# Hybrid mLSTM and dilated-attention layer: order-only edges between PSUM evictions, weight splits and one GpSimd product

## The chip, the cores and the metric

The kernel runs on one core of a Trainium2 chip. A core has five engines that run side by side, each with its own in-order stream of instructions: TensorE (PE in the profile, with PEld for its weight loads), VectorE (DVE), ScalarE (ACT), GpSimd (POOL) and SyncE (SP, which here only issues DMAs). They wait for one another through semaphores. Matrix products land in PSUM, in banks of 128 partitions by 512 floats, and a bank can be used again only after its content has been read out ("evicted") by VectorE or ScalarE. The metric is device time in microseconds of one launch, the median of several runs.

## The reference

One encoder layer is applied to two inputs with shared weights: batch A (x_prompt, 1024 positions) and batch B (x_sample, 512 positions), both 1024 wide. Everything is float32.

```python
h = rms_norm(x, pre_w)
cols = einsum('bsd,dc->bsc', h, w_in)          # one wide projection
m_qk, m_v, m_o, m_z, m_i, m_f, a_qkv, a_z, gate = split(cols)
y_m = mlstm_mixer(m_qk, ...) * silu(m_z)       # 4 heads x 256, forwards and backwards, chunks of 128
y_a = dilated_attention(a_qkv, ...) * silu(a_z) # 3 groups (window, dilation) x 8 heads x 64
p_m, p_a = y_m @ w_pm, y_a @ w_pa
merged = sigmoid(gate[0]) * p_m + sigmoid(gate[1]) * p_a
out = x + rms_norm(merged @ w_out, post_w)
```

`mlstm_mixer` runs a short convolution with SiLU over q and k and then, for each head and direction, a chunked scan. In each chunk the scores q·k are weighted by exponentials of the gates, multiplied with v ("num"), the state matrix's part (q times state) is added, and the state is brought up to date: state = decay * state + k·v ("kv").

## The kernel before, in words

Every float32 product on TensorE is made from three products in a faster 32-bit format: `mm3` (L209 to L211) multiplies high by high, high by low and low by high. So each operand is split first: the high part is a rounded copy, the low part the difference. For weights that is `split_w`, a copy on ScalarE (L272, called wh in the profile) and a subtraction on VectorE (L278, wl). Splits of activations work the same way (Hh and Hl, sch and scl, qh and ql, kh and kl, ch and cl).

*Part 1* (0 to about 950 us). The projection of A and B together, by a scheme with seven products of quarter blocks instead of eight, named B11, T2, B21, T3, T1, T4, B22 in the code. First come the value columns, in groups (`value_group`): the weights' sums are split by its inner `split` (high on ScalarE L477, low on VectorE L478, tiles vhi and vlo). In the first group the sums of the input are still being made beside it by `put` (`combos`): TensorE transposes or adds blocks, ScalarE copies the high part Hh (L432), VectorE subtracts the low part Hl (L434), four column blocks k = 0 to 3 for each sum. While product T3 runs, `with_m7` puts T1's and then T2's input; product T2 comes next and reads it; the split of `s[:, 0]` (`s1`) is for the product after that, T1. In this part the order on all engines but TensorE is made by a scheduler.

*Part 2* (from about 950 us). The order on TensorE and SyncE is written out by hand. Four stages run one after another: `mlstm` for A (to about 1310 us), `attend` for A (to about 1640), `mlstm` for B (to about 1810), `attend` for B (to about 2075), then what is left of the final projections. Each stage has gaps in which TensorE would wait, and these are filled from one queue, `Fill`, with *dense units*: eight steps of `mm3` that add into one PSUM bank (tile `dense`), taken in steps by `fill(share)`. Units are B's remaining projections (`short_units`, with the weights of one 128-column block of w_in each), the value columns (`value_units`), the two branch projections (`branches`) and the output projection (`final`). A unit ends with `use`, which evicts the bank:

- attention's q and k (`att_unit`): high on ScalarE L772, low on VectorE L774
- convolution units: a copy on ScalarE L870 and then `conv_unit` (L735 on ScalarE, L737 and L739 on VectorE)
- SiLU units (`silu`): tanh on ScalarE L746, product on VectorE L749 or L751, the latter also reading a value kept from an earlier unit
- merge gates: tanh on ScalarE L896
- branch projections: VectorE L1643 and L1661
- output projection: square on ScalarE L1704, product on VectorE L1706 or L1711

There are two dense banks (four in the tail), so a third unit cannot begin before the first is evicted. `Fill.load` splits the weights of a unit two to four places ahead of its use; the call that does it comes in program order around the eviction of an earlier unit. The raw weights arrive in `wraw`, loaded on SyncE's queue or (w_pm, w_out and some of w_v) on GpSimd's.

In part 2 the order on ScalarE, VectorE and GpSimd is still the scheduler's, led by its own model of how long things take. `issue_after(x)` adds an edge to it: what is issued in this context comes after x. Such an edge costs no instruction. Some edges stand already: `held` keeps the splits behind the last evictions of the value units and of attention, `scans` keeps the low half of a split behind the last two updates of the mLSTM's state and output.

In `mlstm`, `front(k)` makes a round's operands: `rm` is masked on GpSimd (L1103), exponentiated on ScalarE (L1105) and multiplied with the scores on VectorE (L1106); `sch` (ScalarE L1109) and `scl` (GpSimd L1110) are its halves; `qw` (GpSimd L1114) is q times a row vector that a broadcast load brings (`rw`), and `qh` (ScalarE L1117) and `ql` (GpSimd L1118) are its halves; `kh` (ScalarE L1124) and `kl` (VectorE L1125) are k's. `core(k)` makes the num product, the kv product, updates the state `cf` (VectorE L1149 in a head's first chunk, L1152 later), adds the state's part, and evicts num as X (ScalarE L1167 in the first half of the chunks, VectorE L1169 in the second). `ch` (ScalarE L1176) and `cl` (VectorE L1177) are the state's halves.

## Time and profile before

| | |
|---|---|
| Median of three runs | 2258.14 us (2256.8 to 2259.2) |
| Profiled execution, own time | 2261.5 us |
| Its span in the trace | 2259.7 us |
| TensorE busy | 2244.2 us (99%) |
| VectorE busy | 1509.5 us (67%) |
| ScalarE busy | 1129.2 us (50%) |
| GpSimd busy | 718.6 us (32%) |
| Granted TensorE clock | 1.00 |

The own time of the profiled execution is 1.8 us longer than the span, which goes from the first to the last instruction in the trace. It lies 3.4 us above the median of the runs. A row of the timeline has the start in us, the duration in us, the engine, the line of the kernel, the operation, the result and the operands by the program's names, the shapes and how many of them were joined in the row; in brackets stands the idle time of the engine before it and what ended that. Matmuls are pipelined: of two that follow without a pause the second starts well before the first one's end in the trace, so pauses are read from start to start.

### The profile page before, as it was taken

To read this page: it belongs to the slowest core of one execution; us is meant where nothing else is said; L and a number is where in the kernel's file an instruction comes from. 1 tells how busy PE (TensorE), PEld (TensorE's weight loads), DVE (VectorE), ACT (ScalarE), POOL (GpSimd) and SP (SyncE) were. 2 spreads that over 40 slices of the span, in tenths; PEclk is the share of its full clock that TensorE was granted. 3 is DMA by queue.
4 is the path that set the end of the run, shared out by engine and by line. 5 is a ranking of instruction groups with operands and counts; after the bars stand their busy time and mean duration, and the time that the engine had idled before them with its cause. 6 is when DMAs were issued, how large, how long until landed. Compare 5 with 4: busy or idle time off the path is not lost.

```text
span 2259.7 us, 35388 instructions
## 1 busy us (share of the span) xinstructions
PE 2244.2 (99%) x12226; PEld 1964.6 (87%) x12226; DVE 1509.5 (67%) x2875; ACT 1129.2 (50%) x2369; POOL 718.6 (32%) x1000
## 2 busy tenths in 40 slices
PE   9999999999999999999999999999999999999998
PEld 8999888888888888888888899999888888888887
DVE  7765577687776556558887755544689844655674
ACT  6432244344444434357777655566665644554332
POOL 1000333333333223237676610011165522221221
PEclk9999999999999999999999999999999999999999
DMA  3652455543332223284664789997678797776663
GB/s 123 168 134 76 172 205 192 192 176 121 112 111 103 84 84 140 103 298 153 226 223 127 191 217 235 253 245 221 203 248 284 238 278 211 233 251 200 233 230 109
DMA packets 222685, 418.27 MB, mean 185 GB/s; under 512 B 24841, under 2 KB 128969, under 8 KB 222506
## 3 DMA queue, kind: packets, MB, share of 16 engines
q1 hardware_dynamic: 194536, 315.86, 44.4%
q0 software_dynamic: 24368, 87.56, 12.4%
q10 hardware_dynamic: 3602, 12.59, 1.4%
q8 instruction: 97, 1.59, 0.3%
q14 instruction: 82, 0.67, 0.1%
HBM read 296.19 MB, written 128.12 MB: 188 GB/s over the span
## 4 chain that ended last, share of the span: by engine, by line
PE 95%; DMA 2%; issue 1%; ACT 1%; POOL 1%; DVE 0%; DVEq 0%; SPq 0%; POOLq 0%; ACTq 0%
PE d L211 14%; PE d L209 14%; PE d L210 14%; PE dense L209 12%; PE dense L211 12%; PE dense L210 12%; PE o L1398 4%; PE pt L1385 2%; PE lg L1362 2%; PE num L211 1%; PE num L209 1%; PE num L210 1%; PE kv L209 1%; PE a L1070 1%; PE kv L210 1%
## 5 line engine op out<-in xcount | busy, mean ns | idle before, releaser
L209 PE MATMUL dense<-H,wh 128*128 128x512 f32 x664 | 270.6, 408 | 0.8 <-DVE V0b L1643 0.8
L211 PE MATMUL dense<-H,wl 128*128 128x512 f32 x664 | 260.9, 393 | 0.0
L210 PE MATMUL dense<-H,wh 128*128 128x512 f32 x664 | 260.2, 392 | 0.0
L210 PE MATMUL d<-Hl,phla 128*128 128x512 f32 x608 | 236.5, 389 | 0.0
L211 PE MATMUL d<-Hh,phla 128*128 128x512 f32 x608 | 236.5, 389 | 0.0
L209 PE MATMUL d<-Hh,phla 128*128 128x512 f32 x608 | 236.5, 389 | 0.0
L278 DVE TENSOR_TENSOR wl<-wraw,wh 128x1024 fp32r<-128x1024 f32 (+1 forms) x121 | 149.3, 1234 | 70.0 <-ACT wh L272 69.9
L1374 DVE CUSTOM_DVE_ANT_0 ls<-lg,bias 128x256 f32<-128x256 f32 (+1 forms) x288 | 93.7, 362 | 132.8 <-PE lg L1362 71.2
L211 PE MATMUL d<-Hh,phlb 128*128 128x512 f32 x456 | 177.4, 389 | 0.0
L209 PE MATMUL d<-Hh,phlb 128*128 128x512 f32 x456 | 177.4, 389 | 0.0
L210 PE MATMUL d<-Hl,phlb 128*128 128x512 f32 x456 | 177.4, 389 | 0.0
L687 POOL TENSOR_TENSOR psum_w<-pw_raw 128x512 f32<-128x512 f32 x38 | 58.0, 1527 | 365.1 <-DMA pw_raw<-w_in 208.8
L1378 ACT ACTIVATE ls<-ls,nm 128x256 f32<-128x256 f32 (+1 forms) x288 | 130.3, 454 | 84.0 <-DVE nm L1376 59.2
L272 ACT ACTIVATE wh<-wraw 128x1024 fp32r<-128x1024 f32 (+1 forms) x124 | 128.7, 1038 | 77.1 <-PE dense L210 27.0
L211 PEld LDWEIGHTS dense<-H,wl 128*128 128x128 f32 x664 | 124.6, 188 | 28.2
L209 PE MATMUL d<-vhi,Hh 128*128 128x322 f32 x448 | 140.9, 315 | 0.3
L211 PE MATMUL d<-vhi,Hl 128*128 128x322 f32 x448 | 140.3, 313 | 0.4 <-DVE Hl L396 0.2
L210 PE MATMUL d<-vlo,Hh 128*128 128x322 f32 x448 | 139.7, 312 | 0.0
L209 PEld LDWEIGHTS dense<-H,wh 128*128 128x128 f32 x664 | 125.0, 188 | 15.5 <-DVE V0b L1643 1.2
L210 PEld LDWEIGHTS dense<-H,wh 128*128 128x128 f32 x664 | 125.4, 189 | 14.3
L211 PEld LDWEIGHTS d<-Hh,phla 128*128 128x128 f32 x608 | 114.1, 188 | 23.7
L210 PEld LDWEIGHTS d<-Hl,phla 128*128 128x128 f32 x608 | 114.2, 188 | 23.6
(570 smaller groups left out, 6166.4 us busy)
## 6 DMA issues: line engine op xcount, KB each, us to landing
pw_raw<-w_in SPq DMA_DIRECT2D x76, 512.0 KB
wraw<-w_in SPq DMA_DIRECT2D x64, 512.0 KB
aqk_a<-pwk SPq DMA_DIRECT2D x48, 512.0 KB
aqk_b<-sw SPq DMA_DIRECT2D x48, 256.0 KB
wraw<-w_pm POOLq DMA_DIRECT2D x24, 512.0 KB, 6.1
wraw<-w_out POOLq DMA_DIRECT2D x24, 512.0 KB, 4.0
wraw<-w_v POOLq DMA_DIRECT2D x22, 430.0 KB, 7.3
erep<-erow SPq DMA_DIRECT2D x16, 512.0 KB
```

Of the source, the lines that this page charges most:

```text
L209: nc.tensor.matmul(out, lh, rh, start=start, stop=False)
L210: nc.tensor.matmul(out, lh, rl, start=False, stop=False)
L211: nc.tensor.matmul(out, ll, rh, start=False, stop=stop)
L272: high = nc.scalar.activation(hi[:, :n], raw[:, :n], AF.Copy)
L278: low = (self.lows or nc.vector).tensor_sub(lo[:, :n], raw[:, :n], hi[:, :n].bitcast(F32))
L687: self.nc.gpsimd.tensor_add(s[:, 0], ws[1][:, 0], ws[1][:, 1])
L1070: nc.tensor.matmul(p[:, c - c0], kT[:, ct, c * P:(c + 1) * P], qT[:, ct, c * P:(c + 1) * P], start=ct == 0, stop=ct == 1)
L1362: nc.tensor.matmul(lg[:, hh, c:c + w], q[hh][:, qs], z[:, k0:k0 + w], start=z is k[hh], stop=z is not k[hh])
L1374: nc.vector.tensor_tensor_reduce(out=ls[:, hh], in0=ts["lg"][hh], in1=bt[:, hh], scale=1.0, scalar=NEG, op0=OP.add, op1=OP.max, accum_out= ...
L1378: self.held = self.held[-3:] + [nc.scalar.activation(ls[:, hh], ls[:, hh], AF.Exp, bias=nm[:, hh:hh + 1], accum_out=ot[:, 128 + hh:129 + hh])]
L1385: nc.tensor.transpose(pp[:, hh * nk + x], ts["ls"][:, hh, x * P:(x + 1) * P], self.ident)
L1398: nc.tensor.matmul(po[:, hh * 64:hh * 64 + 64], pt[:, hh * nk + x], v[:, kt[x], c0 + hh * 64:c0 + hh * 64 + 64], start=x == 0, stop=x == n ...
```

## The change

The change adds order edges only; no instruction is added, taken away or altered.

1. Each dense unit notes its eviction's instructions in `self.evicted`, and both halves of the next weight split (`split_w`) are ordered behind them. For the branch projections and the two halves of SiLU only the reads of the bank are noted as shown.
2. In the first eight rounds of an mLSTM stage GpSimd's `qw` is ordered behind `scl`.
3. In the first value group the split of `s[:, 0]` is ordered behind the last copy L432 of T2's input (`top`), beside the edge that it had (`low[2]`, the subtraction of the same block).

```diff
-        self.low_part = None
+        self.low_part, self.evicted = None, []
...
 def split_w(self, raw, n):
...
-            for x in self.held:
+            for x in (*self.held, *self.evicted):
                 st.enter_context(self.tc.issue_after(x.ins))
             high = nc.scalar.activation(hi[:, :n], raw[:, :n], AF.Copy)
...
-                for x in (*self.held, *self.scans):
+                for x in (*self.held, *self.evicted, *self.scans):
                     st.enter_context(self.tc.issue_after(x.ins))
                 low = (self.lows or nc.vector).tensor_sub(lo[:, :n], raw[:, :n], hi[:, :n].bitcast(F32))
...
 def put(m, k):
...
-            nc.scalar.activation(hi, p, AF.Copy)
+            self.high = nc.scalar.activation(hi, p, AF.Copy)
...
             m7 = product(T3, split(wb[:, 0]), with_m7())
+            top = self.high
...
         if g == 0:
-            with self.tc.issue_after(low[2]):
+            with self.tc.issue_after(low[2]), self.tc.issue_after(top.ins):
                 s1 = split(s[:, 0])
...
 def silu(self, c, g, w):
...
-        nc.scalar.activation(th, c, AF.Tanh, scale=0.5)
+        self.evicted = [nc.scalar.activation(th, c, AF.Tanh, scale=0.5)]
         if g is None:
             g = th
-            nc.vector.scalar_tensor_tensor(g, th, 1.0, c, op0=OP.add, op1=OP.mult)
+            self.evicted.append(nc.vector.scalar_tensor_tensor(g, th, 1.0, c, op0=OP.add, op1=OP.mult))
...
 def att_unit(self, j, c, T, w):
...
-            nc.scalar.activation(h, x, AF.Copy, scale=1.0 if keys else 0.125)
+            self.evicted = [nc.scalar.activation(h, x, AF.Copy, scale=1.0 if keys else 0.125)]
...
+            low = nc.vector.scalar_tensor_tensor(l, x, 1.0 if keys else 0.125, h.bitcast(F32), op0=OP.mult, op1=OP.subtract)
+        self.evicted.append(low)
...
 def front(k):
...
-                nc.gpsimd.tensor_sub(scl, rm, sch.bitcast(F32))
+                low = nc.gpsimd.tensor_sub(scl, rm, sch.bitcast(F32))
...
                 if i > 0:
                     qw = sb.tile([P, 2, P], F32, name="qw")
-                    nc.gpsimd.tensor_tensor(qw, ...)
+                    with self.tc.issue_after(low.ins) if k < 8 else ExitStack():
+                        nc.gpsimd.tensor_tensor(qw, ...)
```

In the same way `self.evicted = [...]` is set at the evictions L870 (convolution), L896 (merge gate), L1643 and L1661 (branch projections), and at L1704 with L1706 or L1711 appended (output projection).

More of the change, by code (lines that the diff above doesn't have):

```diff
@@ L771, in att_unit @@
         for h, _, x in parts:
-            nc.scalar.activation(h, x, AF.Copy, scale=1.0 if keys else 0.125)
+            self.evicted = [nc.scalar.activation(h, x, AF.Copy, scale=1.0 if keys else 0.125)]
         for h, l, x in parts:
-            nc.vector.scalar_tensor_tensor(l, x, 1.0 if keys else 0.125, h.bitcast(F32), op0=OP.mult, op1=OP.subtract)
+            low = nc.vector.scalar_tensor_tensor(l, x, 1.0 if keys else 0.125, h.bitcast(F32), op0=OP.mult, op1=OP.subtract)
+        self.evicted.append(low)
         self.put(("aqk", T.S, j), T.aqk[0, j], hi.bitcast(F32), hi)
@@ L869, in use @@
             def use(p):
-                nc.scalar.activation(self.sraw[:, 1:1 + BLK], p, AF.Copy)
+                self.evicted = [nc.scalar.activation(self.sraw[:, 1:1 + BLK], p, AF.Copy)]
                 self.conv_unit(u, T, self.sraw, w, False)
@@ L895, in use @@
                 t = w()
-                nc.scalar.activation(t, p, AF.Tanh, scale=0.5)
+                self.evicted = [nc.scalar.activation(t, p, AF.Tanh, scale=0.5)]
                 self.put(("gt", T.S, br, ct), T.gt[br, ct], t, t)
@@ L1113, in front @@
                     qw = sb.tile([P, 2, P], F32, name="qw")
-                    nc.gpsimd.tensor_tensor(qw, x["q"][:, :, cs], rw[:, 1][:, None, :].to_broadcast([P, 2, P]), op=OP.mult)
+                    with self.tc.issue_after(low.ins) if k < 8 else ExitStack():
+                        nc.gpsimd.tensor_tensor(qw, x["q"][:, :, cs], rw[:, 1][:, None, :].to_broadcast([P, 2, P]), op=OP.mult)
                     qh = sb.tile([P, 2, P], F32R, name="qh")
@@ L1642, in proj_m @@
                     if k == KT - 1:
-                        nc.vector.scalar_tensor_tensor(m2[ct // 4][:, ct % 4], gates.pop((1, ct)), 1.0, pm, op0=OP.add, op1=OP.mult)
+                        self.evicted = [nc.vector.scalar_tensor_tensor(m2[ct // 4][:, ct % 4], gates.pop((1, ct)), 1.0, pm,
+                                                                       op0=OP.add, op1=OP.mult)]
                     yield
@@ L1659, in proj_a @@
                         mg = self.osb.tile([P, BLK], F32, name="mg", bufs=2)
-                        nc.vector.scalar_tensor_tensor(mg, gates.pop((0, ct)), 1.0, pa, op0=OP.add, op1=OP.mult)
+                        self.evicted = [nc.vector.scalar_tensor_tensor(mg, gates.pop((0, ct)), 1.0, pa, op0=OP.add, op1=OP.mult)]
                         nc.vector.tensor_add(mg, mg, m2[ct // 4][:, ct % 4])
@@ L1703, in close @@
                 o1 = sb.tile([P, BLK], F32, name="mg", bufs=2) if u else o[t]
-                nc.scalar.activation(o1, p, AF.Square, accum_out=ss[:, t, u:u + 1])
+                self.evicted = [nc.scalar.activation(o1, p, AF.Square, accum_out=ss[:, t, u:u + 1])]
                 if u == 0:
-                    nc.vector.tensor_mul(o[t], p, pw[:, c])
+                    self.evicted.append(nc.vector.tensor_mul(o[t], p, pw[:, c]))
                     return
@@ L1710, in close @@
                 nc.gpsimd.tensor_tensor(ss[:, t, 6:7], ss[:, t, 5:6], self.mhalf[:, :1], op=OP.pow)
-                nc.vector.tensor_mul(o1, p, pw[:, c])
+                self.evicted.append(nc.vector.tensor_mul(o1, p, pw[:, c]))
                 for hf, x in enumerate((o[t], o1)):
```

## The prediction

> **What bounds the kernel now.** I read the page's first part for the engine that bounds, the list of TensorE's waits for what a new order on the other engines could take away at all, and the timeline around each of those waits.

> ```profile
> PE 2244.2 (99%) x12226; PEld 1964.6 (87%) x12226; DVE 1509.5 (67%) x2875; ACT 1129.2 (50%) x2369; POOL 718.6 (32%) x1000
> L278 DVE TENSOR_TENSOR wl<-wraw,wh 128x1024 fp32r<-128x1024 f32 (+1 forms) x121 | 149.3, 1234 | 70.0 <-ACT wh L272 69.9
> ```

> ```profile
> core 0 of [0], span 2259.7 us
> PE d L1803 <- DMA Hh<-prew: 2.3, 1, 2.3
> PE num L211 <- POOL scl L1110: 1.2, 1, 1.2
> PE kv L209 <- DVE cf L1152: 1.2, 2, 0.6
> PE d L391 <- DVE u2b L389: 0.8, 1, 0.8
> PE dense L209 <- DVE V0b L1643: 0.8, 1, 0.8
> PE dense L209 <- ACT sw L896: 0.7, 1, 0.7
> PE d L438 <- ACT Hh L432: 0.5, 1, 0.5
> PE kv L209 <- DVE r L1163: 0.4, 1, 0.4
> PE o L1398 <- ACT pts L1388: 0.2, 1, 0.2
> PE num L209 <- DVE X L1169: 0.2, 1, 0.2
> PE d L211 <- DVE Hl L396: 0.2, 1, 0.2
> PE kv L209 <- DVE cf L1149: 0.2, 1, 0.2
> PE d L211 <- DVE Hl L434: 0.2, 1, 0.2
> ```

> TensorE works in 2244.2 of 2259.7 us. The second view gives the engine and line that waited, the writer it waited for, the total, the count and the longest. All thirteen together are 8.9 us. No matmul is added, removed or moved by the change, so what it can win is part of these 8.9 us, and what it can lose is a new entry in this list. VectorE and ScalarE have a third and a half of the span free; their order matters only where a result of theirs is late for TensorE.

> **The change part by part.** It adds and removes no instruction. Comparing the two instruction streams, TensorE and the SyncE queue keep their order; VectorE, ScalarE and GpSimd change theirs only in stretches that in the trace of before lie at 50 to 60, 950 to 1350 and 1550 to 1870 us. So 2.3 (start of the tail's first load), 0.8 (L391), 0.5 (L438, at 26 us), 0.4 and the 0.8 of V0b (L1643, at 2026 us) stay: 4.8 of the 8.9. The last of these is worth a word: L1643 is one of the evictions that the change records, but the orders of its neighbours come out the same there.

> *The value group.* On ScalarE the split of the input's last sum, vhi, stands ahead of the last two copies Hh of the product under way:

> ```profile
> 53.23 1.28 ACT L477 ACTIVATE vhi<-vsum 128x1288 fp32r<-128x1288 f32 x1 [1.20 <-PE d L211]
> 54.42 1.06 ACT L432 ACTIVATE Hh<-d 128x512 fp32r<-128x512 f32 x2
> ```

> ```profile
> 54.44 0.31 PE L210 MATMUL d<-vlo,Hh 128*128 128x322 f32 x1
> 54.59 0.31 PE L211 MATMUL d<-vhi,Hl 128*128 128x322 f32 x1
> 55.05 0.41 PE L209 MATMUL d<-vhi,Hh 128*128 128x322 f32 x1
> 55.30 0.31 PE L210 MATMUL d<-vlo,Hh 128*128 128x322 f32 x1
> 55.77 0.41 PE L211 MATMUL d<-vhi,Hl 128*128 128x322 f32 x1 [0.17 <-DVE Hl L434]
> ```

> These matmuls start 0.15 us apart when nothing is late (54.44 to 54.59). The steps 54.59 to 55.05 and 55.30 to 55.77 are 0.46 and 0.47, so 0.31 and 0.32 us too long: a loss of 0.63 us, of which the list names only 0.17. With the copies first they start about 1.2 us earlier (53.23 instead of 54.42), and the loss goes. vhi then starts at about 54.3, 1.1 later, and vlo behind it; the product T1 that reads them begins only after T2's remaining matmuls, some 10 us on, and that work hides it. Gain **0.6**. If the copies are themselves bound by TensorE's transposes (their idle row says 1.20 <-PE), the gain shrinks to 0.3.

> *GpSimd in the mLSTM's first rounds.* In round 5 or so of batch A:

> ```profile
> 994.92 0.31 ACT L1109 ACTIVATE sch<-rm 128x128 fp32r<-128x128 f32 x1 [0.20 <-DVE rm L1106]
> ```

> ```profile
> 997.10 1.19 POOL L1114 TENSOR_TENSOR qw<-Q,rw 128x256 f32<-128x256 f32 x1 [1.68 <-DMA rw<-rw_a]
> 998.25 0.86 POOL L1110 TENSOR_TENSOR scl<-rm,sch 128x128 fp32r<-128x128 f32 x2
> ```

> ```profile
> 997.30 0.28 PE L210 MATMUL num<-V0b,sch 128*128 128x258 f32 x1
> 998.76 0.39 PE L211 MATMUL num<-V0a,scl 128*128 128x258 f32 x1 [1.17 <-POOL scl L1110]
> ```

> scl needs sch, which is there at 994.92 + 0.31 = 995.23. It stands behind qw, which waits for a broadcast load until 997.10 and takes 1.19. With scl ahead, the two of them (0.86 together) run between 995.4 and 996.3, and the matmul at 998.76 follows the one at 997.30 after 0.12 like its kind: 998.76 − 997.42 = **1.3** gained. What it costs: qw is queued behind scl now, up to 0.86 later where its load is early, and qh and ql after it. TensorE reads this round's ql first here, 8 us on, and its dense units in between hide the delay:

> ```profile
> 1005.87 0.28 PE L211 MATMUL num<-ch,ql 128*128 128x258 f32 x1
> ```

> Without that cover it would be 0.86 a round. In batch B no such wait is listed: zero.

> *Evictions ahead of the next split.* At attention's start in batch B:

> ```profile
> 1844.84 1.06 ACT L272 ACTIVATE wh<-wraw 128x1024 fp32r<-128x1024 f32 x1 [4.68 <-DMA wraw<-w_pm]
> 1845.80 0.58 ACT L896 ACTIVATE sw<-dense 128x512 f32<-128x512 f32 x1
> ```

> ```profile
> 1845.32 0.39 PE L211 MATMUL dense<-H,wl 128*128 128x512 f32 x1
> 1846.43 0.50 PE L209 MATMUL dense<-H,X 128*128 128x512 f32 x1 [0.72 <-ACT sw L896]
> ```

> ScalarE stood idle 4.68 us in front of wh for a load while the finished unit's eviction waited behind wh; TensorE ran out of PSUM banks and lost 1846.43 − 1845.32 − 0.23 = **0.9** us. With the eviction first this goes. wh itself comes some 2 to 4 us later, and 16.6 us (1845.90 to 1862.47) of other matmuls stand before the first that reads it:

> ```profile
> 1862.47 0.39 PE L209 MATMUL dense<-V0b,wh 128*128 128x512 f32 x1
> ```

> At the end of batch A's mLSTM the eviction's second half and a split share VectorE with the state's update cf, whose PSUM bank the next kv needs:

> ```profile
> 1280.08 0.69 DVE L749 SCALAR_TENSOR_TENSOR sg<-sg,dense 128x512 f32<-128x512 f32 x1 [0.61 <-ACT sg L746]
> ```

> ```profile
> 1281.08 1.58 DVE L278 TENSOR_TENSOR wl<-wraw,wh 128x1024 fp32r<-128x1024 f32 x1
> ```

> ```profile
> 1283.45 0.74 DVE L1152 SCALAR_TENSOR_TENSOR cf<-cf,rw,kv 128x516 f32<-128x516 f32 x1
> ```

> In the new order L746 and L749 run some 0.6 us earlier (the idle of 0.61 goes), so the chain of wl and cf behind them moves up by up to that: of the two waits of 0.6 for cf, 0.45 of the first and 0.15 of the second, together **0.6**. In batch B's mLSTM the copy of cf (L1149) comes ahead of a product that waits for ScalarE: the 0.2 of its entry.

> What it costs: an eviction that stands ahead of the split is at the head of an in-order queue and waits there for its unit's last matmul. In batch A at 1288 L751 (0.69, as L749) now precedes cf, which has 0.8 us to spare by my reading: 0 to 0.3. At 1087 a convolution unit's two steps move ahead of ch and cl:

> ```profile
> 1087.58 0.82 DVE L1177 TENSOR_TENSOR cl<-cf,ch 128x516 fp32r<-128x516 f32 x1 [0.62 <-ACT ch L1176]
> ```

> ```profile
> 1096.05 0.39 PE L209 MATMUL num<-V1a,sch 128*128 128x258 f32 x1
> ```

> VectorE is then about 0.2 later from there, without a pause up to the sum whose bank that matmul at 1096.05 takes without slack: 0.2 to 0.4. At about ten other places in the mLSTM stages the num or kv bank has under 1 us of slack; I take 0.2 for all of them and 0 to 4 for the range (ten times 0.4). The splits that are moved are ready about as far ahead of their first matmul as the one above (10 to 20 us through the mLSTM stages), so a delay by one eviction (0.58 to 0.69) is hidden by the unit between. A weight buffer is freed later by as much, and the load that waits for it, with what is behind it on its queue, starts later by as much; that load too has a unit's time in hand.

> Splits that land elsewhere on VectorE also change their own length: wl above took 1.58 against a mean of 1.234, beside a GpSimd product. [...]

> **Sum.** Gains 0.6 + 1.3 + 0.9 + 0.6 + 0.2 = 3.6. Losses 0.15 + 0.3 + 0.2 = 0.65. Net −2.95, say −2.9. The profiled execution took 2261.5 us (span 2259.7 and 1.8 around it) and becomes 2258.6. It lies 3.4 above the median of the runs, 2258.14; the same difference from that median gives **2255.2**, 0.13% less. About 0.2% (4.5 us) is what a measurement of this kernel can tell from no change: below 2253.6 is faster, above 2262.7 slower.

> **Rivals.**

> *Faster beyond the bound.* All stalls touched go whole, both waits for cf (1.2) among them, nothing new comes, and some of the small late starts that the list doesn't name go too: 0.6 + 1.3 + 0.9 + 1.2 + 0.2 = 4.2, with 1 us of unlisted ones 5.2, so 2253.0. For it: in the value group the list names 0.17 of 0.63 lost, so such losses exist. Against: the whole list is 8.9, and 4.8 of it lies outside the moved stretches.

> *Slower: the eviction blocks its queue.* On ScalarE and VectorE the eviction now goes ahead of work that would have been ready, and waits for the last matmul of its unit; cf, X or the exponentials stand behind it. Each time that one of them empties a bank with less slack than the eviction's length, TensorE loses about 0.6 (0.58 or 0.69). Six such places cancel the 3.6; twelve, all the tight ones, cost 7.2 and give 2258.1 + 3.6 = 2261.7, and with the exponentials at the end of batch A's attention, which come 1.3 to 2.7 us later at four places, at 0.6 each, 2264.1. For it: at 1087 and 1288 I find the mechanism. Against: in most places the unit is done before the queue reaches its eviction, and the pairs only swap.

> *No effect.* A stall that goes is met again at the next place where TensorE waits for something paced from elsewhere (a load, or a bank fixed by a chain of VectorE work as in the mLSTM): 2258.1. For it: both cf waits at the end of batch A's mLSTM hang on VectorE's chain, so that TensorE, once ahead, can run into the next one. Against: in the stretch around 1.3, 0.9 and 0.6 no other entry of the list lies near.

> **How the numbers follow.** Forecast (2254 to 2257.5) 0.47; no effect 0.13; faster beyond the bound 0.23; slower 0.17, of which 0.1 passes the bound of 0.2%. Of the forecast 0.07 falls below 2253.6. So faster 0.30, slower 0.12, and the rest, 0.58, within. The range that leaves out 1 in 10 on each side goes from the faster rival's far end, 2251.0, to the slower one's, 2262.0.

> **What would show it.** Right: the entries num L211 <-POOL scl and dense L209 <-ACT sw L896 are gone from the list of waits; at 54 us the copies L432 stand before vhi L477 and the matmuls are 0.15 apart; kv <-DVE cf falls from 1.2 to about 0.6; V0b L1643 stays at 0.8; TensorE's busy time is unchanged. Wrong: new entries num <-X, kv <-cf or pt <-ls in the stretches 1090 to 1310 or 1575 to 1870, longer than 3 us together, or a wait dense <-wh or wl, which would say that the splits had less time than I read.

## The result, and the profile after

| | before | after |
|---|---|---|
| Median | 2258.35 us (2256.73 to 2264.08, 20 runs) | 2263.72 us (2262.25 to 2266.81, 20 runs) |
| Ratio after to before | | 1.0021, 95% interval 1.0015 to 1.0027 |
| Profiled execution, own time and span | 2261.5 and 2259.7 us | 2262.36 and 2260.2 us |
| Granted TensorE clock, mean | 1.000 | 0.998 |

The kernel became slower by 5.4 us, 0.24%. The two profiled executions lie only 0.5 us of span apart, because that of before was 3 us above its median and that of after 1.4 below; where the time went is read from the trace, and its size is checked on more runs below.

The list of TensorE's waits after (engine, line, writer: total us, count, longest):

```profile
PE lg L1365 <- DVE ot L1377: 2.6, 1, 2.6
PE d L1807 <- DMA Hh<-prew: 2.4, 1, 2.4
PE pt L1388 <- ACT ls L1381: 1.3, 1, 1.3
...
PE num L209 <- ACT X L1170: 0.7, 1, 0.7
...
```

Lines after the change are 1 to 4 higher than before (L1374 is L1377, L896 is L898, L1167 is L1170, L1594 is L1597). Gone are the entries num <- scl and dense <- sw, which was forecast, and all for cf, which were to halve; the 0.8 for V0b (L1643) and some entries of 0.2 to 0.4 are gone too, which was not forecast. (The 2.3 for Hh, now 2.4, stands in the kernel's first five us and not in the tail, as the prediction has it; nothing in it hangs on that.) New are 2.6 for lg, 1.3 for pt behind it, and 0.7 for num <- X. lg is the score bank of attention, whose reader is the first step of the softmax, L1377 on VectorE.

Around 1855 us, first VectorE before, then VectorE, ScalarE, GpSimd and TensorE after:

```profile
1851.23 1.23 DVE L278 TENSOR_TENSOR wl<-wraw,wh 128x1024 fp32r<-128x1024 f32 x1 [2.01 <-ACT wh L272]
1852.38 0.42 DVE L1374 CUSTOM_DVE_ANT_0 ls<-lg,bias 128x256 f32<-128x256 f32 x1
...
1853.92 1.22 DVE L278 TENSOR_TENSOR wl<-wraw,wh 128x1024 fp32r<-128x1024 f32 x1 [0.56 <-ACT wh L272]
1855.06 0.42 DVE L1374 CUSTOM_DVE_ANT_0 ls<-lg,bias 128x256 f32<-128x256 f32 x1
```

```profile
1848.36 1.77 DVE L278 TENSOR_TENSOR wl<-wraw,wh 128x1024 fp32r<-128x1024 f32 x1 [0.76 <-ACT wh L272]
1855.24 1.23 DVE L278 TENSOR_TENSOR wl<-wraw,wh 128x1024 fp32r<-128x1024 f32 x1 [5.10 <-ACT wh L272]
1856.38 0.42 DVE L1377 CUSTOM_DVE_ANT_0 ls<-lg,bias 128x256 f32<-128x256 f32 x1
```

```profile
1833.11 0.63 ACT L1597 ACTIVATE K<-ymr 128x512 fp32r<-128x512 f32 x1 [5.78 <-DMA ymr<-ym_a]
1833.65 0.58 ACT L898 ACTIVATE sw<-dense 128x512 f32<-128x512 f32 x1
1834.12 1.05 ACT L272 ACTIVATE X<-wraw 128x1024 fp32r<-128x1024 f32 x1
...
1854.15 1.06 ACT L272 ACTIVATE wh<-wraw 128x1024 fp32r<-128x1024 f32 x1 [5.33 <-DMA wraw<-w_pm]
```

```profile
1836.73 0.53 POOL L261 DMA_DIRECT2D wraw<-w_pm  x1 [1.42 <-DVE X L278]
...
1847.90 0.53 POOL L261 DMA_DIRECT2D wraw<-w_pm  x1 [4.16 <-DVE wl L278]
```

```profile
1853.65 1.00 PE L1401 MATMUL o<-X,pts 128*128 128x64 f32 x8
1857.30 0.71 PE L1365 MATMUL lg<-V1a,Q 128*128 128x256 f32 x4 [2.65 <-DVE ot L1377]
1859.27 1.18 PE L1388 MATMUL pt<-ident,ls 128*128 128x128 f32 x4 [1.26 <-ACT ls L1381]
...
1861.10 0.63 PE L211 MATMUL dense<-H,Q 128*128 128x512 f32 x1
```

Before, a softmax step followed each of the two splits. After, VectorE goes from the split at 1848.36 straight to the next one and stands idle 5.10 us in front of it: its high half wh is copied only at 1854.15, for ScalarE itself waited 5.33 us for a w_pm load issued at 1847.90. The softmax step behind it, which needs nothing from that split, starts at 1856.38. Counted from the start of the stage it is the fourth, the one that before stood at 1852.38, between the two splits: the change put it behind the second of them. TensorE needs the bank that it reads. From the output products to lg it takes 3.65 us (1853.65 to 1857.30) instead of 0.81, and from there to pt 1.97 (to 1859.27) instead of 0.56.

The pauses are not all. The windows of before and after the change (stretch, its length, the busy time of TensorE, its weight loads, VectorE, ScalarE and GpSimd, then granted clock, DMA share, GB/s):

```profile
1854.00:1858.00 4.00, 4.00 (x25) 3.48 (x24) 2.43 (x6) 1.51 (x6) 0.53 (x1) 1.00 1.00 297
1858.00:1862.00 4.00, 4.00 (x27) 3.62 (x26) 0.35 (x1) 1.06 (x1) 0.00 (x0) 1.00 1.01 272
```

```profile
1854.00:1858.00 4.00, 1.35 (x10) 1.05 (x9) 2.76 (x10) 1.71 (x3) 0.53 (x1) 1.00 0.69 193
1858.00:1862.00 4.00, 2.74 (x10) 2.15 (x10) 1.90 (x5) 3.39 (x10) 0.00 (x0) 0.54 0.92 282
1862.00:1866.00 4.00, 4.00 (x13) 3.15 (x12) 3.01 (x8) 4.00 (x11) 3.71 (x7) 0.61 0.82 288
```

After the pauses the granted clock is 0.54 and 0.61 for two windows, and matmuls of 128 x 512 start 0.43 us apart instead of 0.23 (row 1861.10 lasts 0.63 instead of 0.39). The missing clock, (0.46 + 0.39) x 4, is 3.4 us, and the trace has the clock at 0.50 for 6.83 us. TensorE's progress through 1850 to 1880 shows what both cost: 7.1 us more than before, some 4.2 of it standing (the two steps above, less those of before) and the other 2.9 at the lower clock.

The whole comparison by stretches is worked out from the starts of the same matmuls in both traces: the time that TensorE took for a stretch of its instruction stream, less what it took in the first trace of before. "Before again" is a second trace of the unchanged kernel (first experiment) and shows how far one trace is from another; "after again" is a second trace of the change (seventh).

| Stretch of before (us) | before again | after | after again |
|---|---|---|---|
| 20 to 245 (value group) | +1.2 | -0.5 | -0.6 |
| 955 to 1070 (scl ahead of qw) | -0.4 | -1.4 | -1.5 |
| 1070 to 1110 (convolution) | -0.1 | +1.0 | +1.4 |
| 1270 to 1310 (end of A's mLSTM) | -1.0 | -2.0 | -2.0 |
| 1310 to 1640 | -0.5 | -0.3 | -0.5 |
| 1640 to 1800 (B's mLSTM) | -0.9 | -1.4 | -1.4 |
| 1830 to 1850 (eviction ahead of wh) | +0.6 | -1.0 | -1.0 |
| **1850 to 1880** | **0.0** | **+7.1** | **+7.8** |
| 1990 to 2040 | -0.9 | -1.0 | -0.8 |
| 2110 to 2140 (tail) | +0.3 | +0.1 | +0.2 |

One place costs 7 to 8 us; everything else together is 6.6 us faster than the first trace of before and about 4 faster than the second. In the medians the rest is worth 7.1 or 7.8 less 5.4, so about 2.

### The profile page after: what moved, and what is told of

It reads as the page before. It is cut to its first block, busy times and chain, and to the rows that moved or that the text cites. A ratio compares the mean times of both kernels' runs of the same rounds, so it can differ in the third digit from the quotient of the medians.

```text
span 2260.2 us, 35332 instructions
## 1 busy us (share of the span) xinstructions
PE 2245.0 (99%) x12226; PEld 1966.8 (87%) x12226; DVE 1508.8 (67%) x2875; ACT 1125.0 (50%) x2369; POOL 717.9 (32%) x1000
## 4 chain that ended last, share of the span: by engine, by line
PE 94%; DMA 2%; issue 1%; DVE 1%; ACT 1%; POOL 0%; DVEq 0%; POOLq 0%; SPq 0%; ACTq 0%
PE d L211 13%; PE d L209 13%; PE d L210 13%; PE dense L209 12%; PE dense L211 12%; PE dense L210 12%; PE o L1401 4%; PE pt L1388 2%; PE lg L1365 2%; PE num L209 1%; PE num L211 1%; PE num L210 1%; PE a L1072 1%; DMA vs_a<-vz 1%; PE kv L210 1%
## 5 line engine op out<-in xcount | busy, mean ns | idle before, releaser
L209 PE MATMUL dense<-H,wh 128*128 128x512 f32 x664 | 270.5, 407 | 0.0
L211 PE MATMUL dense<-H,wl 128*128 128x512 f32 x664 | 260.9, 393 | 0.0
L210 PE MATMUL dense<-H,wh 128*128 128x512 f32 x664 | 260.1, 392 | 0.0
L210 PE MATMUL d<-Hl,phla 128*128 128x512 f32 x608 | 236.5, 389 | 0.0
L211 PE MATMUL d<-Hh,phla 128*128 128x512 f32 x608 | 236.5, 389 | 0.0
L209 PE MATMUL d<-Hh,phla 128*128 128x512 f32 x608 | 236.5, 389 | 0.0
L278 DVE TENSOR_TENSOR wl<-wraw,wh 128x1024 fp32r<-128x1024 f32 (+1 forms) x121 | 149.6, 1237 | 57.9 <-ACT wh L272 57.1
L1377 DVE CUSTOM_DVE_ANT_0 ls<-lg,bias 128x256 f32<-128x256 f32 (+1 forms) x288 | 93.4, 361 | 126.4 <-PE lg L1365 67.0
L211 PE MATMUL d<-Hh,phlb 128*128 128x512 f32 x456 | 177.4, 389 | 0.0
L209 PE MATMUL d<-Hh,phlb 128*128 128x512 f32 x456 | 177.4, 389 | 0.0
L210 PE MATMUL d<-Hl,phlb 128*128 128x512 f32 x456 | 177.4, 389 | 0.0
L272 ACT ACTIVATE wh<-wraw 128x1024 fp32r<-128x1024 f32 (+1 forms) x124 | 128.6, 1037 | 56.1 <-DMA wraw<-w_pm 14.6
L211 PEld LDWEIGHTS dense<-H,wl 128*128 128x128 f32 x664 | 124.7, 188 | 28.3
L209 PE MATMUL d<-vhi,Hh 128*128 128x322 f32 x448 | 140.8, 314 | 0.1
L211 PE MATMUL d<-vhi,Hl 128*128 128x322 f32 x448 | 140.2, 313 | 0.2 <-DVE Hl L396 0.2
L210 PE MATMUL d<-vlo,Hh 128*128 128x322 f32 x448 | 139.7, 312 | 0.2 <-DVE vlo L478 0.2
L210 PEld LDWEIGHTS dense<-H,wh 128*128 128x128 f32 x664 | 125.3, 189 | 14.3
L209 PEld LDWEIGHTS dense<-H,wh 128*128 128x128 f32 x664 | 125.0, 188 | 14.3
L211 PEld LDWEIGHTS d<-Hh,phla 128*128 128x128 f32 x608 | 114.1, 188 | 23.7
L210 PEld LDWEIGHTS d<-Hl,phla 128*128 128x128 f32 x608 | 114.1, 188 | 23.7
```

What stands on the lines that cost most here:

```text
L209: nc.tensor.matmul(out, lh, rh, start=start, stop=False)
L210: nc.tensor.matmul(out, lh, rl, start=False, stop=False)
L211: nc.tensor.matmul(out, ll, rh, start=False, stop=stop)
L272: high = nc.scalar.activation(hi[:, :n], raw[:, :n], AF.Copy)
L278: low = (self.lows or nc.vector).tensor_sub(lo[:, :n], raw[:, :n], hi[:, :n].bitcast(F32))
L1377: nc.vector.tensor_tensor_reduce(out=ls[:, hh], in0=ts["lg"][hh], in1=bt[:, hh], scale=1.0, scalar=NEG, op0=OP.add, op1=OP.max, accum_out= ...
```

## The experiments

In each group the kernel before ran on the same chip. The first four ask which edges cause the loss at 1855, and by which way.

**The kernel before again.** No edit.

> The kernel before, unchanged, for a second trace. Its profiled execution was 3.4 us above its median, and I moved that difference over to the changed kernel as if it were constant. If the excess sits in some of the waits that the prediction took as gains, this trace (own time near 2258) lacks some of them: the list of TensorE's waits should then come to about 5.5 instead of 8.9 us, the 1.2 at scl being the likeliest to be absent, as it hung on a load. If the excess sits outside the trace's waits, the list is again 8.9 with the same entries. Time 2258.4, ratio 1.000.

Measured: 2259.35 us (11 runs), ratio 0.9999 (0.9991 to 1.0008). Its waits are not those of the first trace: the entries for V0b and for cf at L1152 (1.2) are absent, the one for scl is 0.8 instead of 1.2, the one for sw 1.3 instead of 0.7, and the list comes to 7.8 instead of 8.9. Waits of about 1 us and less come and go between executions of one kernel, so the vanished V0b wait says nothing about the change, and the vanished ones for cf say little.

**No edges in batch B's attention.** The edges of part 1 are left out from the last stage on.

```diff
-            for x in (*self.held, *self.evicted):
+            for x in (*self.held, *(self.evicted if self.behind else ())):
...
+            N.behind = False     # ahead of attend(B)
```

> The whole change, but from batch B's attention on no split is ordered behind an eviction. Theory (order in batch B's attention): the two waits lg <- VectorE 2.6 and pt <- ScalarE 1.3 at 1854 to 1860 us and the lowered clock behind them go, together 6.6 us by the traces' start times; the 0.9 at L896 returns; 2263.7 - 6.6 + 0.9 = 2258.0. Rival (the loss in the median is spread over the mLSTM and attention A stages, where most edges are): the time stays within 1 us of 2263.7 and the waits there grow.

Measured: 2260.65 us (11 runs), ratio 1.0003 (0.9994 to 1.0012). There is no wait for lg and the 7 us at 1850 to 1880 fall to 1.0. In their place comes the wait for an eviction, 3.5 us in three pieces:

```profile
PE dense L209 <- ACT sw L898: 3.5, 3, 1.9
```

So the edges of this stage cause the loss, and without them something else is lost. In two of the pieces the eviction stands behind a split; in the longest, 1.9, it stands on ScalarE behind K, which waited 5.14 us for its load. The change has no wait there. Why these waits are longer here than in the kernel before is not shown.

**Without one edge.** The edges left out are those of one split, the 99th, tile X in the rows above. With them the split stands at 1834.12 behind the eviction L898 and so behind K, which had waited 5.78 us for its load.

```diff
+        n_th, self.count = self.count, self.count + 1
+        ev = self.evicted if n_th != 98 else ()
...
-            for x in (*self.held, *self.evicted):
+            for x in (*self.held, *ev):
```

> The whole change without the edges of one split: the 99th, of a merge gate's weights, which the change puts behind a copy (L1594) that waits for a load on GpSimd's queue. GpSimd's order of loads then is that of before, and the third split of w_pm stands behind the softmax's first step on VectorE again, while the eviction L896 still precedes the split at 1845 us. Theory: no wait at 1854, clock 1.000, and the gains stay: 2263.7 - 6.6 = 2257, with the 0.9 at L896 gone too. Rival (any of the other edges in this stage causes it): still a wait of 2 us or more for lg, 2262 to 2264.

Measured: 2258.74 us (11 runs), ratio 0.9997 (0.9988 to 1.0006). The changed kernel, measured against the same kernel before in the next group, is at 2265.38: the edges of this one split are worth 6.6 us. ScalarE, GpSimd and VectorE of this run (its lines are two higher again):

```profile
1829.43 1.05 ACT L274 ACTIVATE X<-wraw 128x1024 fp32r<-128x1024 f32 x1
...
1835.68 0.63 ACT L1599 ACTIVATE K<-ymr 128x512 fp32r<-128x512 f32 x1 [5.20 <-DMA ymr<-ym_a]
...
1851.08 1.06 ACT L274 ACTIVATE wh<-wraw 128x1024 fp32r<-128x1024 f32 x1 [0.68 <-DMA wraw<-w_pm]
```

```profile
1832.22 0.53 POOL L261 DMA_DIRECT2D wraw<-w_pm  x1 [0.60 <-DVE X L280]
```

```profile
1847.72 0.42 DVE L1379 CUSTOM_DVE_ANT_0 ls<-lg,bias 128x256 f32<-128x256 f32 x1 [0.73 <-POOL bias L1341]
...
1849.94 1.23 DVE L280 TENSOR_TENSOR wl<-wraw,wh 128x1024 fp32r<-128x1024 f32 x1 [1.44 <-ACT wh L274]
1852.17 1.23 DVE L280 TENSOR_TENSOR wl<-wraw,wh 128x1024 fp32r<-128x1024 f32 x1 [0.92 <-ACT wh L274]
1853.31 0.42 DVE L1379 CUSTOM_DVE_ANT_0 ls<-lg,bias 128x256 f32<-128x256 f32 x1
```

X is split ahead of K instead of behind it. That frees its raw buffer early: the w_pm load that waits for the buffer is issued at 1832.22 instead of 1836.73, and two loads later the split's high half stands at 1851.08 instead of 1854.15. The edges of this one split also move VectorE's order, as expected: the step at 1847.72 is the fourth softmax step, the one that TensorE waited for after the change, and here it stands ahead of both splits. The one behind them, at 1853.31, is the fifth. So this version takes away the bad order and the late weights at once, and does not say by itself which of the two the 6.6 us hang on. The clock stays at 1.000.

**Without another edge.** The edges of the 97th split, two before, are left out instead; then GpSimd issues ym and w_pm loads in the order of before, although the edges of the 99th are there.

```diff
+        ev = self.evicted if n_th != 96 else ()
```

> The whole change without the edges of the 97th split. GpSimd's order of loads is that of before here too, but VectorE has the third split of w_pm still ahead of the softmax's first step. Theory D (the order on VectorE is what costs: a split that waits for its load stands ahead of the lg bank's reader): the wait lg <- VectorE is still there, 1 to 3 us, and the time 2260 to 2264. Theory P (the weight's load was issued too late on GpSimd, behind a load of ymr): with its queue as before the split is in time and the wait goes: about 2257.

Measured: 2259.05 us (11 runs), ratio 1.0000 (0.9991 to 1.0009). In the profiled execution (2261.49, 2.4 above this median) the wait remains and is shorter:

```profile
PE lg L1367 <- DVE ot L1379: 1.9, 1, 1.9
```

```profile
1856.86 1.23 DVE L280 TENSOR_TENSOR wl<-wraw,wh 128x1024 fp32r<-128x1024 f32 x1 [3.36 <-ACT wh L274]
1858.00 0.42 DVE L1379 CUSTOM_DVE_ANT_0 ls<-lg,bias 128x256 f32<-128x256 f32 x1
```

So the order of the loads on GpSimd's queue is not the cause by itself. The step at 1858.00 is again the fourth, behind the third split of w_pm (the one whose load is late) as after the change. This order on VectorE is what parts the eleven traces without added pauses: it stands in all four that have the wait for lg (the change twice, this version, and part 1 alone below) and in none of the seven others, in which the fourth step comes ahead of the third split. How long TensorE then stands depends on when that split's weights land: it waited 1.9, 2.6 and 4.7 us where VectorE had stood 3.36, 5.10 and 6.77 us in front of the split (this version, the change, part 1 alone). An estimate: with the third split at 1853.92, as before, and the steps of after (1.14 from it to the softmax step, 0.92 from there to lg), lg would have come at 1855.98 instead of 1854.16. So the order alone would cost about 1.8 us of wait with the loads of before; after the change the split is 1.3 us later and the wait 2.8. No version has the bad order and early weights. The stretch costs 3.6 us here: 1.9 waiting and 1.7 at the lower clock (0.63 and 0.95 in the windows of 4 us from 1858 on, as above (0.37 + 0.05) x 4).

The next four take the change apart by its own parts.

**Only parts 2 and 3** (scl ahead of qw, and the value group; `self.evicted` is noted but not used).

```diff
-            for x in (*self.held, *self.evicted):
+            for x in self.held:
...
-                for x in (*self.held, *self.evicted, *self.scans):
+                for x in (*self.held, *self.scans):
```

> Parts 2 and 3 alone: scl ahead of qw in the first rounds, and the value group's split behind the copies; no split behind an eviction. Theory (each gain is real and stays): 0.6 in the value group and 1.0 to 1.3 at 997 us, so 1.6 to 1.9 below before. Rival (a lead is met again at the next place that something else paces): the gain at 997 shrinks by 1094 us, where VectorE's chain sets the num bank, or in batch B's attention between 1825 and 1870, where the DMA engines are full; then within 0.5 us of before.

Measured: **2256.47 us** (11 runs), ratio 0.9988 (0.9979 to 0.9996): 2.7 us faster than before.

**Only part 1.** The two other edges are left out.

> Part 1 alone: splits behind evictions, scl and the value group as before. Theory: the stretch 1850 to 1880 us is again about 7 us longer, so about 1.7 above the whole change: before + 5 to 7. Rival (the loss needs the lead that parts 2 and 3 bring, as TensorE then arrives earlier at loads that come when they come): the stretch is 1.5 to 2 us shorter than with the whole change and the time is that of the whole change or below, before + 4.

Measured: 2267.84 us (5 runs), ratio 1.0038 (1.0025 to 1.0051): 8.7 us slower. The wait for lg is the longest of all, 4.7 us, and the clock falls behind it as after the change:

```profile
1861.15 1.23 DVE L278 TENSOR_TENSOR wl<-wraw,wh 128x1024 fp32r<-128x1024 f32 x1 [6.77 <-ACT wh L272]
```

```profile
1862.00:1866.00 4.00, 2.01 (x8) 1.55 (x9) 2.50 (x12) 1.48 (x5) 0.53 (x1) 0.56 0.72 234
```

**The change again.** No edit to the changed kernel.

> The changed kernel itself, for a second trace and its time beside the other experiments. Theory: 1850 to 1880 us is 6 to 8 us longer than before again, with the waits lg <- VectorE and pt <- ScalarE and the lowered clock; 4 to 5 us above before. If the first trace's stall was an accident of its loads, this one is shorter and the time is nearer to before.

Measured: 2265.38 us (9 runs), ratio 1.0028 (1.0018 to 1.0038), with a wait for lg of 3.9 and the clock at 0.998. The loss is the change's, not one execution's.

**A few edges.** Parts 2 and 3, and part 1 only at seven splits: 36 and 37 (end of A's mLSTM), 98 and 100 to 103 (batch B's attention, without the two in question).

```diff
+        ev = self.evicted if n_th in (35, 36, 97, 99, 100, 101, 102) else ()
```

> Parts 2 and 3, and of part 1 only the edges of the splits at the end of batch A's mLSTM (the 36th and 37th) and at the start of batch B's attention (the 98th and the 100th to 103rd), so without those around 1080 to 1094 us and without the 97th and 99th. Theory: the losses of 1.0 at 1070 to 1110 and of 7 at 1850 to 1880 go, the gains of 0.6, 1.0 to 1.3, 1.0 and 0.9 stay: 3 to 3.5 below before, the fastest of all. Rival (the leads are given back where the DMA engines are full): within 1 us of before, with a new wait between 1825 and 1870.

Measured: 2256.62 us (11 runs), ratio 0.9992 (0.9983 to 1.0000). It is as fast as parts 2 and 3 alone: the edges kept gain nothing that can be measured in the time. The trace shows 1.1 us less at 1270 to 1310 than with parts 2 and 3 alone, and a wait at 1743 in batch B's mLSTM that neither the kernel before nor the change has:

```profile
1743.30 0.38 PE L209 MATMUL kv<-V0a,kh 128*128 128x258 f32 x1 [1.04 <-DVE cf L1157]
```

**Without three edges.** All of the change but the edges of the 99th split and of the 15th and 16th, which stand beside the convolution at 1080 to 1096.

```diff
+        ev = self.evicted if n_th not in (14, 15, 98) else ()
```

> The changed kernel without part 1's edges at three of its 133-odd splits: the two in batch A's early mLSTM (the 15th and 16th split, beside the convolution at 1080 to 1096) and the 99th, at attention's start in batch B. Theory A (the loss is in these two places only: the late softmax step with the pause and the lowered clock behind it, 7.1 to 7.8, and the later sum X, 1.0 to 1.4): no wait lg<-ot near 1857 and no num<-X near 1095, the clock at 1.000, and a time of 2265.4 - 7.1 - 1.2 = 2257.1, between the kernel before (2259.2) and the version without any edge of part 1 (2256.5). Theory B (part 1 costs a little at many places): at least 2260, above before.

Measured: 2257.66 us (11 runs), ratio 0.9993 (0.9984 to 1.0002), with no wait for lg or X and a clock of 1.000. The time is the one expected from the two places alone, and not the 2260 of many small losses. But the stretch 1070 to 1110 is not free: the wait for X has gone and the kv product at 1081 now starts 0.95 us late, so 0.6 of the 1.0 remain. And, as in the version without edges in this stage, a wait stands at 1836 for an eviction that ScalarE reaches only after K has waited 5.37 us for its load:

```profile
1836.74 0.50 PE L209 MATMUL dense<-H,wh 128*128 128x512 f32 x1 [1.91 <-ACT sw L900]
```

The last two ask whether the lower clock belongs to the pauses. Both are the kernel before with pauses put into batch A's attention: after a value unit's last matmul a small matmul waits for a copy chain, so only TensorE and a little of GpSimd and VectorE is touched.

```diff
+    def pause(self, bank, m):
+        nc.vector.tensor_copy(z[0], bank[:, :8])
+        for i in range(m):
+            nc.gpsimd.tensor_copy(z[(i + 1) % 2], z[i % 2])
+        nc.tensor.matmul(bank[:8, :8], z[m % 2], z[m % 2], start=True, stop=True)
```

**Seven pauses** (m = 2, 5, 8, ... 20).

> The kernel before with seven pauses of TensorE put by hand into batch A's attention, where the DMA engines are not full: after a value unit's last matmul a small copy chain of 2, 5, 8, ... 20 steps runs on GpSimd from the finished bank, and a small matmul (8 by 8, into the bank that has been read) waits for its end. Nothing else is changed. It costs the pauses themselves, some 1 to 4 us each. Theory A (a long enough pause of TensorE lowers the granted clock by itself): the windows behind the longer pauses show a clock of 0.5 to 0.7 for some 4 us and the matmuls there start 0.43 apart, behind the shorter ones 1.00 and 0.23, with the border near 2 to 2.5 us. Theory B (the clock fell at 1858 for another reason, the full DMA engines or the kind of matmul): 1.00 behind all pauses up to 3 us.

Measured: 2314.05 us in one run. The seven pauses are 2.6 to 8.0 us from start to start, longer than planned, and behind every one of them the clock is 0.50 for a while. The one of 4.6 us, with DMA engines idle when TensorE resumes (the windows give TensorE's busy time alone):

```profile
1464.21 0.18 PE L874 MATMUL dense<-z 128*8 128x8 f32 x1 [4.29 <-POOL z L873]
```

```profile
1460.00:1464.00 4.00, 0.00 (x0) 0.90 0.76 204
1464.00:1468.00 4.00, 3.79 (x16) 0.50 0.01 2
1468.00:1472.00 4.00, 4.00 (x25) 0.74 0.64 164
```

So the clock fell here at a pause put in by hand, with a DMA share of 0.76 in the window before TensorE resumes and 0.01 in the next; full DMA engines were not needed for it.

**Ten short pauses** (m = 0 or 1).

> The same as the kernel with pauses, but ten of them, with 0 or 1 step on GpSimd instead of 2 to 20, so about 2.0 to 2.5 us long by the steps of 0.25 us (2.78 with 2 steps). Theory A (a pause lowers the clock from some length on, near 2.6 us): no drop behind any of them, and a cost of ten times about 2.1, 21 us, in all. Theory B (whether a pause of this length counts depends on where it falls in a stretch that the chip watches, so that at the same length some are followed by 0.5 and some are not): a drop behind two to five of the ten, each worth 1.7 to 2 us more. Theory C (2 us suffice): a drop behind all ten, 40 us in all.

Measured: 2283.19 us in one run. The ten are 1.2 to 3.1 us long. Seven leave the clock at 1.00 (1.2, 1.5, 1.5, 1.8, 2.0, 2.0 and 2.55), three lower it (2.07, 2.20 and 3.1). The 2.07 and the 2.55:

```profile
1421.37 0.17 PE L874 MATMUL dense<-z 128*8 128x8 f32 x1 [1.72 <-DVE z L871]
1446.08 0.17 PE L874 MATMUL dense<-z 128*8 128x8 f32 x1 [2.20 <-POOL z L873]
```

```profile
1421.00:1425.00 4.00, 3.63 (x18) 0.59 1.05 362
1425.00:1429.00 4.00, 4.00 (x30) 0.99 0.57 149
1441.00:1445.00 4.00, 2.88 (x21) 1.00 1.06 239
1445.00:1449.00 4.00, 2.92 (x22) 1.00 1.05 237
1449.00:1453.00 4.00, 4.00 (x29) 1.00 0.74 177
```

The longer of the two leaves no trace and the shorter one costs (0.41 + 0.01) x 4 = 1.7 us. So length alone does not part these two. The packed trace has the time of each change of the clock: here 1421.70, 1425.11, 1469.49, 1472.90, 1493.38 and 1500.21. The later ones lie 1, 14, 15, 21 and 23 steps of 3.413 us behind the first (78.51 us over the 23), so all six lie on one grid. On this grid the pause of 2.07 lies within one step (1418.28 to 1421.70), and the one of 2.55 is divided at 1445.59 into 2.07 and 0.48, of which the first begins with the last matmul's own 0.2 us. That a pause counts by how much of it falls in one step is my reading of these two; what sets the times is not shown.

## Why the prediction was wrong

The forecast was 2255.2 in 2251.0 to 2262.0; measured 2263.7, so slower instead of faster. Point by point:

*The gains* were there as waits. num <- scl is gone and its stretch is 1.4 to 1.5 faster in both traces (forecast 1.3; 1.1 against the second trace of before). dense <- sw is gone, 1.0 (forecast 0.9). At the end of A's mLSTM all waits for cf are gone, 2.0 against the first trace and 1.0 against the second (forecast 0.6), in which the two of L1152 are absent as well. In the value group the order is the one forecast:

```profile
53.63 1.08 ACT L432 ACTIVATE Hh<-d 128x512 fp32r<-128x512 f32 x2 [1.57 <-PE d L428]
54.60 1.28 ACT L477 ACTIVATE vhi<-vsum 128x1288 fp32r<-128x1288 f32 x1
```

The copies come 0.8 earlier and not 1.2, since TensorE's transposes bound them (1.57 <-PE in the row), the case for which the text gave 0.3 instead of 0.6. The traces can't size that: the stretch is 0.5 faster than in the first trace of before, 1.7 faster than in the second. Parts 2 and 3 alone, forecast at 1.9, gave 2.7 with an interval that holds 1.9. For part 1 the traces show the waits gone, but the time does not: without the 99th split's edges the kernel is at 2258.74 and 2257.66, against 2256.47 for parts 2 and 3 alone. The intervals overlap; that part 1's other edges gain anything is not shown.

*The step that failed* is the last one under costs: "A weight buffer is freed later by as much, and the load that waits for it, with what is behind it on its queue, starts later by as much; that load too has a unit's time in hand." In batch B's attention it has none. "By as much" was wrong first: X's split was not delayed by one eviction (0.58) but by K, which the eviction stood behind and which waited 5.78 us for a load of its own. Its high half comes at 1834.12 instead of 1832.08, the w_pm load that waits for its buffer at 1836.73 instead of 1834.69, and the third split 1.3 us later than before. The cover was wrong second, and this weighs more: I looked at who reads the split on TensorE (10 to 20 us later, and there was indeed no wait for wh or wl), but not at who stands behind the split on VectorE. With the edges this was the fourth softmax step, which had stood ahead of that split, and TensorE needed its bank at once. The loss for it in the sum was nothing; it measured 4.2 us of standing. The working had compared the instruction streams and named 1550 to 1870 us as a stretch where VectorE's order changes, but put no price on this swap. Why the scheduler swaps the two for edges at an earlier split is not shown. The split that waited for its load held up VectorE for 5.10 us. The trace of before showed the material: the load that ended ScalarE's idle time of 4.68 in this very stage, and a DMA share of 1.00.

*The lower clock* was in no term. Of the 7.1 us some 2.9 are not the wait but what the wait did to the clock, 0.50 for 6.83 us.

*A mis-sized term:* the convolution at 1087, taken at 0.2 to 0.4. The stretch lost 1.0 and 1.4 in the two traces, 0.8 of it in both at the sum named, and 0.3 and 0.5 at a kv product at 1082, ahead of it. The mechanism was the right one, and the entry num <- X came where it was looked for. ScalarE after:

```profile
1085.88 0.80 ACT L736 ACTIVATE sw<-sraw,cws 128x512 f32<-128x512 f32 x1
1086.58 0.62 ACT L1179 ACTIVATE ch<-cf 128x516 fp32r<-128x516 f32 x1
```

The two before, in the other order:

```profile
1086.91 0.63 ACT L1176 ACTIVATE ch<-cf 128x516 fp32r<-128x516 f32 x1
1087.44 0.81 ACT L735 ACTIVATE sw<-sraw,cws 128x512 f32<-128x512 f32 x1
```

ch is only 0.33 earlier than before, while TensorE, having gained at 998, is 1.5 to 1.7 earlier: L736 ahead of ch took most of the lead, and X comes 0.9 too late for it. I had reckoned VectorE's delay against the old arrival of TensorE, not against the one that my own gain of 1.3 gave. The experiment without these edges removes the wait for X, but there the kv product loses 0.95, so 0.6 of the loss stays.

*The rivals.* "The eviction blocks its queue" had the right sign, and its range, to 2264.1, holds the result, but not by its mechanism: no eviction that waits for its unit's matmuls cost much. "No effect", a lead that is met again, fits part 1's gains in the version with a few edges and in the one without three, which both have new waits (at 1743 and 1836); that these take the gains is not shown.

*The signs* would not have found the loss: the new entries num <- X and pt <- ls come to 2.0 us, under the 3 that the text asked for, and lg is not among those it names. In the numbers, no sum gives the range's lower end, 2251.0, as the faster rival's own ends at 2253.0; the chances give 0.1 for slower beyond the bound and then 0.12; and the wl of 1.58 ran beside two subtractions of GpSimd (ql and scl), not a product.

*The carry-over* of 3.4 between the profiled execution and the median held for before only; the profiled execution of after lies 1.4 below its median. Forecasts of a few us should be made as differences, not from one execution's own time.

*The bound to tell from no change*, 0.2%, was about right: the result, 0.21% by the ratio, is just told apart.

## What to carry to other kernels

For an instruction that is to move behind another, follow the whole chain in front of it on its engine to the last load, and then everything that stands behind it, on the other engine of a pair (high, low) too: its own reader's slack is not the only one that counts. Where the order is a scheduler's, compare it before and after on every engine, and look for a reader of a PSUM bank that has landed behind an instruction that waits for a load; here one such swap was worth more than all gains. Parts of a change are worth measuring alone: parts 2 and 3 are 2.7 us faster than before, and the edges of one split in part 1 bring more than the whole loss.
